# Thirty-two experts of 64 slots each become sixteen pairs that share 64 slots

## The chip, the cores and the metric

The kernel runs on one core of one Trainium2 chip. The core has five engines with a queue of instructions each: TensorE (PE; the loads of its stationary operand are shown apart, as PEld), VectorE (DVE), ScalarE (ACT), GpSimd (POOL) and SyncE (SP, which here issues the weight loads). Sixteen DMA engines move data between memory (HBM) and the core. A matmul writes into PSUM, from where VectorE or ScalarE fetches the result; all else lives in SBUF, 128 partitions of it. The metric is the device time of the whole program in microseconds. Before the change three runs took 1750.53, 1749.68 and 1748.38 us; the median is 1749.68 us.

## The reference

Two transformer blocks over 256 tokens of 1024 features. Block 1 is a mixer (mLSTM and gMLP), a cross attention and a mixture of 32 experts; block 2 has two layers, each with three mixers (a long convolution through a spectrum, gated linear attention, pooling) and a feed-forward part. The change is within the mixture of experts. Cut to what matters:

```python
def hier_moe(h, w_rg, b_rg, w_re, b_re, w_gate, w_up, w_down):
    p_group = jax.nn.softmax(h @ w_rg + b_rg)               # 4 groups of 8 experts
    p_top, g_idx = lax.top_k(p_group, 1)                    # each token goes to one group
    e_logits = (h @ w_re + b_re).reshape(T, 4, 8)           # ... and there
    e_top, e_local = lax.top_k(e_logits[own group], 2)      # to two experts
    weights = p_top * jax.nn.softmax(e_top)
    expert_id = g_idx * 8 + e_local
    ...
    y = (silu(xb @ w_gate[e]) * (xb @ w_up[e])) @ w_down[e] # the tokens xb of expert e
    return sum over a token's two experts of weights * y
```

The gate and up matrices of an expert are 1024 x 512, its down matrix is 512 x 1024, all fp32. All 32 experts have to be read, 201 MB, whatever the routing; 512 places (256 tokens, two experts each) are spread over them. Experts j and j + 16 are never in the same group, so no token goes to both.

## The kernel before

*Weights.* Each weight is used as hi + lo, two parts of 12 significant bits, in matmuls of the type fp32r. The experts' weights come as 192 loads of 1 MiB (raw, 128 x 2048), issued by SyncE, 9 of which can be in SBUF at once. A load is two chunks of 1024 columns. For each chunk ScalarE makes the hi part (whi, line 450) and VectorE the lo part (wlo, line 451, raw - whi). There are 5 buffers for hi parts and 4 for lo parts (NH, NL in the code), so that splits run at most five chunks ahead of TensorE. A load's place comes free when both its chunks are split.

*Slots.* Each expert has 64 slots. `rank` counts for every token how many tokens before it go to the same expert; that rank is its slot. Tokens beyond the 64th would be dealt with in a loop over all tokens, `beyond`, which makes no trips where all have a slot. `chosen` makes the one-hot Dm of token and slot for four experts on VectorE (line 849); `features` gathers with it 128 features of the tokens in those slots, for four experts at once, on TensorE (line 861), and ScalarE copies them into XT (line 864). The stationary operand of an expert's matmul is 128 features x 128: 64 slots of the token's hi part and 64 of its lo part. So one pass of whi and one of wlo gives rows 0 to 63 from the hi tokens and rows 64 to 127 from the lo tokens, and the two halves are added later.

*An expert* has 12 chunks, one a step: 4 for gate, 4 for up (`up`, lines 938 and 939), 4 for down (`down`, lines 954 and 955), with four matmuls of 512 columns each. Gate goes into a PSUM tile `misc`, of which there are two; ScalarE copies its lower half (z, line 885), VectorE adds the upper (line 887), and ScalarE makes SiLU of it twice, for both halves of g (line 891). Up goes into the other `misc` tile and VectorE multiplies it into g (line 895). `fold` adds the two halves of g and transposes in one go: four matmuls with a constant of stacked identity matrices (line 902), into a PSUM tile `tp` (also two); ScalarE and VectorE split that into at, hi and lo (lines 906 and 908). Down runs over at into two `tp` tiles, each copied to ye by ScalarE (line 913). `combine` takes ye back to the tokens: for each token tile and each half of the features one fp32 matmul (line 919) with DT, the weights of tokens in slots, accumulating in the four `acc` tiles over all experts. DT comes from `weighted`: VectorE multiplies Dm by the tokens' weights (Dw, line 873), TensorE transposes four 128 x 128 blocks (line 878), ScalarE copies (line 880).

*The order* is written out by hand. Each piece of work is a Python generator; `plan[step]` lists what is started at a step, a generator yields the number of steps until its next part, and `go_on` runs at each step those that are due, ahead of the step's four matmuls. `WHEN` and `DOWN` are tables of the steps: the features of the next four experts, their slots and weights, and one step of block 2's filters for nearly every expert (24 such steps, lines 1265 to 1290; all but four of them beside the experts). Gate and up of expert e are followed by down of expert e - 1, whose fold is started in step 2 of expert e; the combinations of expert e - 2 stand in steps 4 to 7.

All engines keep this order within the mixture of experts. What stands before it (its norm and the router) and after it (the last sums, two norms and block 2) is ordered by the same program in both kernels.

Of the kernel before, what the change touches and what calls it, by code (L numbers as in the profile page):

```python
# [22 lines left out]
F32 = mybir.dt.float32  # L23
# [8 lines left out]
P = 128  # L32
D = 1024
S = 256
# [45 lines left out]
# after which expert's first products an expert's last one follows: the next one's, but for those of the end,  # L80
# so that no expert's middle is waited for there
DOWN = lambda e: () if e in (0, NE - 2) else (e - 1,) if e < NE - 1 else (NE - 3,) if e == NE - 1 else (NE - 2, NE - 1)
# which of four experts, and which of its 12 steps: for 128 features of the next four each, their slots, their
# weights; and the steps for the filters of block 2
WHEN = dict(features=((1, 1), (1, 4), (1, 5), (1, 7), (3, 5), (3, 6), (3, 7), (4, 0)), chosen=(0, 2),
            weighted=((1, 8), (1, 9)), filters=(7, 7, 8, 2))
def _constants():
    """Tables by where they are needed, and what is where in them."""
# [5 lines left out]
        "cst": dict(ident=np.eye(P), fold=np.concatenate([np.eye(SLOTS)] * 2), slot=np.arange(SLOTS)[None] - BIG,  # L94
# [17 lines left out]
def _tables():  # L112
    """Constants of the second block that depend on its shapes alone."""
# [35 lines left out]
def _short(a):  # L149
    """Rounded to 12 significant bits."""  # L150
# [5 lines left out]
# tables of numbers of at most 12 significant bits  # L156
# [6 lines left out]
def _prepare(i):  # L163
    """Only layout: what the program reads, by name."""
# [32 lines left out]
    gu = np.stack([i["w_gate"][0], i["w_up"][0]], 1).reshape(NE, 2, 4, 2, P, 512)  # L197
    o["w_egu"] = _pairs(gu.transpose(0, 1, 2, 4, 3, 5).reshape(NE * 8, P, 1024))
    dn = i["w_down"][0].reshape(NE, 2, 2, P, 2, 512)
# [44 lines left out]
# ------------------------------------------------------------------- program  # L244

class Kernel:
# [13 lines left out]
    def weights(self, name, n, parts=None):  # L260
        """Chunk n of a weight as hi + lo, each of 12 significant bits."""
# [19 lines left out]
    def load(self):  # L281
        """The next load of the stream."""
# [11 lines left out]
    def ahead(self, n):  # L294
        """The first n chunks of the stream, split."""
# [8 lines left out]
    def constants(self, name, pool, w=0):  # L304
        """A table of constants, or the first columns of it (the rest is to be loaded by load_rest)."""
# [29 lines left out]
    def room(self, pool, tags):  # L335
        """Tiles for the parts of a chunk: one of both, or one of each (None: the usual one)."""
# [25 lines left out]
    def dense_t(self, xT, name, chunks, consume):  # L362
        """Columns of those chunks (128 each, at most two): consume(psum[128, n, 256])."""
# [9 lines left out]
    # ---- norms and transposes  # L373
# [7 lines left out]
    def squares(self, halves):  # L381
        """Sum of squares over both halves, as two columns."""
# [7 lines left out]
    def rsqrt(self, v, w=1):  # L390
        """v^-1/2 of a [128, w]."""
# [4 lines left out]
    def inv_norm(self, ss):  # L396
        """(sum + n eps)^-1/2: the inverse rms over sqrt(n) = 32."""
# [4 lines left out]
    def gained(self, x, g, out, n):  # L402
        """out = 32 x g, half n."""
# [3 lines left out]
    def to_T(self, src, hi, lo, t, k0=0, n=8):  # L407
        """src [128 tok, n * 128] of token tile t -> hi, lo [128, k0:k0+n, tok]; without lo, hi is the whole."""
# [16 lines left out]
    def norm(self, gname, pool, tag, g=None):  # L425
        """Tiles for rms_norm(x) g as hi, lo [128, 8, tok], and what fills them from a token tile."""
# [21 lines left out]
    def split(self, hi, lo, src):  # L448
        """hi + lo = src, each of 12 significant bits."""
# [3 lines left out]
    # ---- everything  # L453
# [37 lines left out]
    # ---- block 1: mixer, cross attention  # L491

    def block1(self, outer, moe):
# [3 lines left out]
        with ExitStack() as ctx:  # L497
# [33 lines left out]
            # gates: i_f at 0.., i_b at 32.., f_f at 64.., f_b at 96..  # L531
# [40 lines left out]
            # q, k: [128 of the head, head, tok]  # L572
# [16 lines left out]
            # E[s, t] = exp(u_s - M_t) where s reaches t  # L589
# [53 lines left out]
            # output gate and gu wait in y for what they multiply  # L643
# [9 lines left out]
            # gMLP  # L653
# [39 lines left out]
            # memory side of the cross attention does not wait for the mixer  # L693
# [22 lines left out]
            for e in range(NE + 1):  # L716
                if e < NE:
                    self.stream.extend(("w_egu", 4 * e + n) for n in range(4))
# [949 lines left out]
```

## Time and profile before

| | |
|---|---|
| runs | 1750.53, 1749.68, 1748.38 us |
| span of the profiled execution | 1747.4 us |
| TensorE busy in the span | 1689.9 us, 97% |
| VectorE | 1310.1 us, 75% |
| ScalarE | 1185.6 us, 68% |
| HBM traffic | 415.96 MB, mean 238 GB/s |
| mixture of experts, first gate matmul to last down matmul | 260.7 to 839.8 us, 579.1 us |

The profile is of one execution; its span of 1747.4 us lies 2.3 us under the median of the runs. A row of the timeline gives the start, the duration, the engine, the line, the operation, the result and what it is made from, and the shape; [in brackets] stands the idle time ahead of it and what ended that. Each fp32 matmul (lines 902 and 919) has two records, "x2" for one. Matmuls are pipelined: the next one starts before the record of the last one ends, so what one costs is read from the distance of two starts rather than from its duration. In the table of stretches a busy time stands for each engine, then the granted clock of TensorE as a share of 2.4 GHz, then the mean busy share of the DMA engines and what they moved.

### The profile page before, as it was taken

To read this page: it belongs to the slowest core of one execution; us is meant where nothing else is said; L and a number is where in the kernel's file an instruction comes from. 1 tells how busy PE (TensorE), PEld (TensorE's weight loads), DVE (VectorE), ACT (ScalarE), POOL (GpSimd) and SP (SyncE) were. 2 spreads that over 40 slices of the span, in tenths; PEclk is the share of its full clock that TensorE was granted. 3 is DMA by queue.
4 is the path that set the end of the run, shared out by engine and by line. 5 is a ranking of instruction groups with operands and counts; after the bars stand their busy time and mean duration, and the time that the engine had idled before them with its cause. 6 is when DMAs were issued, how large, how long until landed. Compare 5 with 4: busy or idle time off the path is not lost. (4 is left out here: it accounts for less than half of the span.)

```text
span 1747.4 us, 25396 instructions
## 1 busy us (share of the span) xinstructions
PE 1689.9 (97%) x9401; PEld 1421.2 (81%) x9401; DVE 1310.1 (75%) x1697; ACT 1185.6 (68%) x1672; POOL 30.4 (2%) x47
## 2 busy tenths in 40 slices
PE   7999978999999999999899999999999999999998
PEld 6898866777777777777589987899878998789986
DVE  7976568889888989999558867677655786667763
ACT  7865439889888889999557655555545765555552
POOL 1000000000000000000000000000000000000000
PEclk9999989999999999999999999999999999999999
DMA  8645537989899999998566456455656645645551
GB/s 286 210 165 192 192 140 271 354 337 362 333 344 350 358 346 369 372 388 335 175 211 222 147 187 215 149 184 185 212 178 210 233 142 188 202 152 183 185 192 69
DMA packets 94451, 415.96 MB, mean 238 GB/s; under 512 B 12324, under 2 KB 18868, under 8 KB 68468
## 3 DMA queue, kind: packets, MB, share of 16 engines
q1 hardware_dynamic: 89220, 405.91, 65.4%
q0 software_dynamic: 864, 6.29, 1.0%
q10 hardware_dynamic: 4240, 2.10, 0.4%
q8 instruction: 75, 1.23, 0.3%
q14 instruction: 52, 0.43, 0.1%
HBM read 411.12 MB, written 3.15 MB: 237 GB/s over the span
## 5 line engine op out<-in xcount | busy, mean ns | idle before, releaser
L451 DVE TENSOR_TENSOR wlo<-raw,whi 128x1024 fp32r<-128x1024 f32 x709 | 851.6, 1221 | 234.4 <-PE acc L328 82.9
L450 ACT ACTIVATE whi<-raw 128x1024 fp32r<-128x1024 f32 x711 | 733.0, 1054 | 203.4 <-PE acc L329 119.9
L332 PE MATMUL acc<-hl,whi 128*128 128x256 f32 x1024 | 290.1, 283 | 0.0
L333 PE MATMUL acc<-hh,wlo 128*128 128x256 f32 x1024 | 290.1, 283 | 0.0
L331 PE MATMUL acc<-hh,whi 128*128 128x256 f32 x1024 | 289.9, 283 | 0.0
L938 PE MATMUL misc<-whi,XT 128*128 128x512 f32 x512 | 241.3, 471 | 2.1 <-DVE z L887 1.3
L939 PE MATMUL misc<-wlo,XT 128*128 128x512 f32 x512 | 203.4, 397 | 2.5 <-DVE wlo L451 2.1
L331 PEld LDWEIGHTS acc<-hh,whi 128*128 128x128 f32 x1024 | 196.7, 192 | 0.1
L332 PEld LDWEIGHTS acc<-hl,whi 128*128 128x128 f32 x1024 | 196.7, 192 | 0.0
L333 PEld LDWEIGHTS acc<-hh,wlo 128*128 128x128 f32 x1024 | 196.7, 192 | 0.0
L939 PEld LDWEIGHTS misc<-wlo,XT 128*128 128x128 f32 x512 | 97.1, 190 | 44.4 <-issue 15.8
L919 PE MATMUL acc<-ye,DT 128*128 128x512 f32 x256 | 129.5, 592 | 0.0
L938 PEld LDWEIGHTS misc<-whi,XT 128*128 128x128 f32 x512 | 96.9, 189 | 39.6 <-issue 21.6
L327 PE MATMUL acc<-whi,hh 128*128 128x512 f32 x288 | 113.5, 395 | 0.6 <-ACT hh L418 0.5
L328 PE MATMUL acc<-wlo,hh 128*128 128x512 f32 x288 | 113.5, 395 | 0.1
L329 PE MATMUL acc<-whi,hl 128*128 128x512 f32 x288 | 112.8, 392 | 0.0
L954 PE MATMUL tp<-whi,at 128*128 128x512 f32 x256 | 110.1, 430 | 1.5 <-ACT XT L864 1.2
L955 PE MATMUL tp<-wlo,at 128*128 128x512 f32 x256 | 100.6, 393 | 0.4 <-DVE wlo L451 0.4
L327 PEld LDWEIGHTS acc<-whi,hh 128*128 128x128 f32 x288 | 54.5, 189 | 12.8 <-ACT hh L418 1.2
L329 PEld LDWEIGHTS acc<-whi,hl 128*128 128x128 f32 x288 | 54.5, 189 | 11.9 <-DVE hl L419 0.8
L328 PEld LDWEIGHTS acc<-wlo,hh 128*128 128x128 f32 x288 | 54.4, 189 | 11.3 <-DVE wlo L451 0.5
L954 PEld LDWEIGHTS tp<-whi,at 128*128 128x128 f32 x256 | 48.1, 188 | 18.0 <-issue 4.2
(459 smaller groups left out, 2847.9 us busy)
## 6 DMA issues: line engine op xcount, KB each, us to landing
raw<-in_w_egu SPq DMA_DIRECT2D x128, 1024.0 KB
raw<-in_w_ed SPq DMA_DIRECT2D x64, 1024.0 KB
raw<-in_w_up SPq DMA_DIRECT2D x80, 512.0 KB
raw<-in_w_gate SPq DMA_DIRECT2D x48, 512.0 KB
raw<-in_w_down SPq DMA_DIRECT2D x44, 512.0 KB
raw<-in_w_qk SPq DMA_DIRECT2D x24, 512.0 KB
raw<-in_w_out SPq DMA_DIRECT2D x24, 512.0 KB
raw<-in_w_br SPq DMA_DIRECT2D x24, 512.0 KB
```

The costliest lines, as they stand in the source:

```text
L327: mm(out, xh, wh, start=start, stop=False)
L328: mm(out, xh, wl, start=False, stop=False)
L329: mm(out, xl, wh, start=False, stop=stop)
L331: mm(out, wh, xh, start=start, stop=False)
L332: mm(out, wh, xl, start=False, stop=False)
L333: mm(out, wl, xh, start=False, stop=stop)
L450: self.nc.scalar.activation(hi, src, AF.Copy)
L451: self.nc.vector.tensor_sub(lo, src, hi.bitcast(F32))
L919: mm(sums[t][n], DT[e // 4][:, e % 4, t * P:(t + 1) * P], Y[e, n], start=e == 0, stop=e == NE - 1)
L938: mm(p, l, wh[:, c], start=h == k == 0, stop=False)
L939: mm(p, l, wl[:, c], start=False, stop=h == 3 and k == 1)
L954: mm(p, l, wh[:, c], start=h == k == 0, stop=False)
```

## The change

Experts j and j + 16 make a pair. The pair has one set of 64 slots: the tokens of the first member come first, those of the second behind them (in `rank`, two more matmuls add the first member's count to the second member's ranks, and `mine` marks which of the rows belong to the first). Each member's XT holds its own tokens in their slots and zeros in the other slots. So gate of the first and gate of the second can accumulate into one `misc` tile over 8 chunks, up likewise, and one copy, one sum, two SiLU and one product serve both. `fold` gets a moving operand of 128 columns instead of 64, F: the stacked identities with only the first member's rows, and with only the second's. VectorE makes F for each pair (lines 915 and 916), two steps ahead of the fold's matmuls. So `at` has both members' hidden features, zeros in the other's slots, and down of both accumulates in one `misc` tile (before: `tp`) over 4 chunks for each half of the features. Two ye copies and four combinations follow for each pair. `weighted` makes Dw for two pairs at a time, with small VectorE operations from the slot numbers and two small tables (rp, wp), two steps before its transposes instead of six. A step of the plan is still one chunk; a pair has 24 steps, and a load is still 1 MiB, two chunks. The loads come in the new order of the chunks. The numbers of buffers NH, NL and the 9 places stay.

The diff, without what only removes comments:

```diff
+PAIRS = NE // 2
+MEMBERS = [m * PAIRS + j for j in range(PAIRS) for m in range(2)]
+WHEN = dict(features=((0, 6), (0, 9), (0, 12), (0, 15), (1, 14), (1, 16), (1, 18), (1, 20)), chosen=2,
+            weighted=(1, 4, 7, 10), filters=(8, 14), combine=(3, 5, 7, 9))
+DOWN = lambda j: (j - 1,) if j else ()
...
+            rp, wp = (a.tile([P, 2, PAIRS], F32, name=k) for k in ("rp", "wp"))
+            r2 = rk.rearrange("p t (j m) -> p t j m", m=2)
+            nc.vector.tensor_tensor(rp, r2[:, :, :, 0], r2[:, :, :, 1], op=OP.min)
+            nc.vector.tensor_add(wp, W[:, :, :PAIRS], W[:, :, PAIRS:])
...
+            def weighted(o, t, h):
+                Dw = a.tile([P, 2, 2, SLOTS], F32, name="Dw")
+                for n in range(2):
+                    j = 4 * o + 2 * h + n
+                    nc.vector.tensor_scalar(Dw[:, n], self.c["slot"][:, None, :].to_broadcast([P, 2, SLOTS]),
+                                            rp[:, t, j:j + 1], wp[:, t, j:j + 1], op0=OP.is_equal, op1=OP.mult)
+                yield 2
                 ps = self.tp()
-                for e in range(4):
-                    nc.tensor.transpose(ps[:, e * P:(e + 1) * P], Dw[:, e].rearrange("p i j -> p (i j)"), self.ident)
+                for n in range(2):
+                    nc.tensor.transpose(ps[:, n * P:(n + 1) * P], Dw[:, n].rearrange("p i j -> p (i j)"), self.ident)
                 yield 1
...
-            def fold(e):
-                g = G.pop(e)
+            def fold(j):
+                F = a.tile([P, 2, SLOTS], F32, name="F")
+                nc.vector.tensor_scalar(F[:, 0], self.c["fold"], mine[:, j:j + 1], None, op0=OP.mult)
+                nc.vector.tensor_sub(F[:, 1], self.c["fold"], F[:, 0])
+                yield 2
+                g = G.pop(j)
                 pt = self.tp()
                 for f in range(4):
-                    mm(pt[:, f * SLOTS:(f + 1) * SLOTS], g[:, f * P:(f + 1) * P], self.c["fold"], start=True, stop=True)
+                    mm(pt[:, f * P:(f + 1) * P], g[:, f * P:(f + 1) * P], F.rearrange("p m j -> p (m j)"),
+                       start=True, stop=True)
...
                 for i in range(2):
                     p = self.misc()
-                    for h in range(4):
+                    for s in range(8):
+                        m, h = divmod(s, 4)
                         go_on()
-                        wh, wl = self.weights("w_egu", 8 * e + 4 * i + h)
+                        wh, wl = self.weights("w_egu", 16 * j + 8 * m + 4 * i + h)
                         for k in range(2):
-                            l = XT[q][h][:, k, r].rearrange("p i j -> p (i j)")
+                            l = XT[q][h][:, k, 2 * r + m].rearrange("p i j -> p (i j)")
                             c = slice(k * 512, k * 512 + 512)
-                            mm(p, l, wh[:, c], start=h == k == 0, stop=False)
-                            mm(p, l, wl[:, c], start=False, stop=h == 3 and k == 1)
+                            mm(p, l, wh[:, c], start=s == k == 0, stop=False)
+                            mm(p, l, wl[:, c], start=False, stop=s == 7 and k == 1)
...
-                    p = self.tp()
-                    for h in range(2):
+                    p = self.misc()
+                    for s in range(4):
+                        m, h = divmod(s, 2)
                         go_on()
-                        wh, wl = self.weights("w_ed", 4 * e + 2 * n + h)
+                        wh, wl = self.weights("w_ed", 8 * j + 4 * m + 2 * n + h)
...
+                if j < PAIRS:
+                    plan[0].append(fold(j - 1))
+                if j == 1 or j % 4 == 3 and j < PAIRS - 1:
+                    for n, s in enumerate(WHEN["weighted"]):
+                        plan[s].append(weighted((j + 1) // 4, n // 2, n % 2))
...
+            plan[WHEN["combine"][2 * n + t]].append(combine(j - 2, t, n))
```

Two places of the order show how instructions move. The first is VectorE around the fold of one expert, in the second half of the stage, before the change; lines 451, 908, 887 and 895 are the lo part, the lo part of at, the gate's sum and the product with up.

```order
L451 TENSOR_TENSOR wlo<-raw,whi 128x1024 x8
L908 TENSOR_TENSOR at<-tp,at 128x4x64
L451 TENSOR_TENSOR wlo<-raw,whi 128x1024
L887 TENSOR_TENSOR z<-misc,z 64x512
L451 TENSOR_TENSOR wlo<-raw,whi 128x1024 x3
L895 TENSOR_TENSOR g<-g,misc 128x512
```

The same place after it, for one pair; lines 455, 929, 901 and 909 are the same operations, 915 and 916 make F.

```order
L909 TENSOR_TENSOR g<-g,misc 128x512
L455 TENSOR_TENSOR wlo<-raw,whi 128x1024 x9
L915 TENSOR_SCALAR F<-cst,mine 128x64
L916 TENSOR_TENSOR F<-cst,F 128x64
L455 TENSOR_TENSOR wlo<-raw,whi 128x1024 x3
L929 TENSOR_TENSOR at<-tp,at 128x8x64
L455 TENSOR_TENSOR wlo<-raw,whi 128x1024 x5
L901 TENSOR_TENSOR z<-misc,z 64x512
```

Between two products with up there are now 24 lo parts instead of 12, and the two operations for F stand three lo parts ahead of at's subtraction, which follows the fold's matmuls.

The second place is TensorE between combinations, in the middle of the stage. Before, one chunk, that is four weight matmuls (lines 938 and 939), stand between two combinations (line 919):

```order
L919 MATMUL acc<-ye,DT 128x512
L938 MATMUL misc<-whi,XT 128x512
L939 MATMUL misc<-wlo,XT 128x512
L938 MATMUL misc<-whi,XT 128x512
L939 MATMUL misc<-wlo,XT 128x512
L919 MATMUL acc<-ye,DT 128x512
```

After, with lines 960 and 961 for the weight matmuls and 940 for the combination:

```order
L940 MATMUL acc<-ye,DT 128x512
L960 MATMUL misc<-whi,XT 128x512
L961 MATMUL misc<-wlo,XT 128x512
L960 MATMUL misc<-whi,XT 128x512
L961 MATMUL misc<-wlo,XT 128x512
L960 MATMUL misc<-whi,XT 128x512
L961 MATMUL misc<-wlo,XT 128x512
L960 MATMUL misc<-whi,XT 128x512
L961 MATMUL misc<-wlo,XT 128x512
L940 MATMUL acc<-ye,DT 128x512
```

Now two chunks of weights, eight matmuls, stand between two combinations instead of one chunk with four, and there are four combinations in 24 chunks instead of four in 12.

## Rows read from the trace of the kernel before

**Rows 1.** The page: its first line and TensorE's line of busy time.

```profile
span 1747.4 us, 25396 instructions
...
PE 1689.9 (97%) x9401; PEld 1421.2 (81%) x9401; DVE 1310.1 (75%) x1697; ACT 1185.6 (68%) x1672; POOL 30.4 (2%) x47
```

**Rows 2.** Stretches: us, busy PE, PEld, DVE, ACT, POOL, clock, DMA share, GB/s.

```profile
260.70:298.00 37.30, 32.29 (x149) 25.64 (x149) 28.38 (x30) 33.02 (x44) 0.00 (x0) 0.90 0.73 261
298.00:633.10 335.10, 329.22 (x1526) 247.95 (x1525) 293.47 (x297) 292.74 (x388) 0.00 (x0) 1.00 0.93 347
633.10:799.10 166.00, 164.97 (x737) 125.29 (x736) 158.04 (x156) 158.92 (x204) 0.00 (x0) 1.00 0.97 375
799.10:839.80 40.70, 40.01 (x161) 27.96 (x160) 37.25 (x37) 33.96 (x42) 0.00 (x0) 1.00 0.57 234
380.00:390.00 10.00, 10.00 (x44) 7.37 (x43) 7.49 (x9) 6.59 (x8) 0.00 (x0) 1.00 1.00 396
430.00:440.00 10.00, 10.00 (x49) 7.52 (x48) 9.09 (x9) 9.92 (x14) 0.00 (x0) 1.00 1.00 391
780.00:805.00 25.00, 25.00 (x111) 19.26 (x109) 24.82 (x25) 23.94 (x30) 0.00 (x0) 1.00 1.00 398
281.60:285.00 3.40, 3.40 (x13) 3.02 (x14) 1.90 (x3) 1.79 (x3) 0.00 (x0) 0.50 0.86 318
```

**Rows 3.** Stretches of line 885 alone: busy ScalarE and count of copies, then as above.

```profile
298.00:633.10 335.10, 10.71 (x18) 1.00 0.93 347
633.10:799.10 166.00, 5.95 (x10) 1.00 0.97 375
```

**Rows 4.** TensorE's timeline around two combinations: start, us, operation.

```profile
510.98 1.02 PE L919 MATMUL acc<-ye,DT 128*128 128x512 f32 x2
511.44 0.79 PE L938 MATMUL misc<-whi,XT 128*128 128x512 f32 x1
512.07 0.39 PE L939 MATMUL misc<-wlo,XT 128*128 128x512 f32 x1
...
512.77 1.02 PE L919 MATMUL acc<-ye,DT 128*128 128x512 f32 x2
```

**Rows 5.** TensorE's timeline around a fold.

```profile
504.77 0.39 PE L939 MATMUL misc<-wlo,XT 128*128 128x512 f32 x1
505.00 1.00 PE L902 MATMUL tp<-cst,g 128*128 128x64 f32 x8
505.81 0.48 PE L938 MATMUL misc<-whi,XT 128*128 128x512 f32 x1
506.12 0.39 PE L939 MATMUL misc<-wlo,XT 128*128 128x512 f32 x1
```

**Rows 6.** VectorE's timeline in a late expert.

```profile
781.41 9.34 DVE L451 TENSOR_TENSOR wlo<-raw,whi 128x1024 fp32r<-128x1024 f32 x8
790.66 0.42 DVE L908 TENSOR_TENSOR at<-tp,at 128x256 fp32r<-128x256 f32 x1
791.00 1.22 DVE L451 TENSOR_TENSOR wlo<-raw,whi 128x1024 fp32r<-128x1024 f32 x1
792.13 0.67 DVE L887 TENSOR_TENSOR z<-misc,z 64x512 f32<-64x512 f32 x1
792.73 2.34 DVE L451 TENSOR_TENSOR wlo<-raw,whi 128x1024 fp32r<-128x1024 f32 x2
```

**Rows 7.** Groups by line and shape, 298 to 799.1 us: count, busy, mean, idle before.

```profile
L939 PEld LDWEIGHTS misc<-wlo,XT 128*128 128x128 f32 x448 | 84.5, 189 | 41.5 <-issue 14.8 <-DVE wlo L451 12.2 <-DVE Dm L849 1.0
...
L873 DVE TENSOR_TENSOR Dw<-Dm,W 128x512 f32<-128x512 f32 x13 | 8.9, 685 | 0.0
L878 PE MATMUL tp<-cst,Dw 128*128 128x128 f32 x56 | 8.8, 280 | 3.3 <-ACT DT L880 3.2
...
L1285 DVE MEMSET fk<- 1x128 f32 x6 | 1.0, 165 | 1.0 <-ACT fk L1281 0.9
```

**Rows 8.** TensorE's timeline, two waits within the first two experts.

```profile
275.81 0.47 PE L938 MATMUL misc<-whi,XT 128*128 128x512 f32 x1 [1.30 <-DVE z L887]
...
280.09 0.50 PE L861 MATMUL tp<-Dm,hh 128*128 128x256 f32 x2 [2.19 <-DVE Dm L849]
```

More of the change, by code (lines that the diff above doesn't have):

```diff
@@ L93, in _constants @@
     tables = {
-        "cst": dict(ident=np.eye(P), fold=np.concatenate([np.eye(SLOTS)] * 2), slot=np.arange(SLOTS)[None] - BIG,
+        "cst": dict(ident=np.eye(P), fold=np.concatenate([np.eye(SLOTS)] * 2), row=(s % SLOTS)[:, None], slot=np.arange(SLOTS)[None] - BIG,
                     idx=np.arange(NE)[None] - BIG, tri=s[:, None] < s[None, :]),
@@ L941, in up, with down @@
+                            mm(p, l, wl[:, c], start=False, stop=s == 7 and k == 1)
+                        for work in plan[8 * i + s]:
                             start(work)
-                    start(gated(e, p) if i else gate(e, p))
-            def down(e, plan):
-                at = AT.pop(e)
+                    start(gated(j, p) if i else gate(j, p))
+            def down(j, plan):
+                at = AT.pop(j)
                 for n in range(2):
-                    p = self.tp()
-                    for h in range(2):
+                    p = self.misc()
+                    for s in range(4):
+                        m, h = divmod(s, 2)
@@ L956, in down @@
-                        for work in plan[8 + 2 * n + h]:
+                            mm(p, l, wh[:, c], start=s == k == 0, stop=False)
+                            mm(p, l, wl[:, c], start=False, stop=s == 3 and k == 1)
+                        for work in plan[16 + 4 * n + s]:
                             start(work)
-                    start(result(e, n, p))
+                    start(result(j, n, p))
             def flush():
@@ L966, in moe @@
             todo = deque(twice(w) for w in spectra[:1] * 12 + spectra[1:] * 12)
-            last = NE // 4 - 1
+            last = PAIRS // 2 - 1
             start(chosen(0))
@@ L972, in moe @@
             go_on()
[L973 to L976 removed]
+            for j in range(PAIRS + 1):
+                q, r = divmod(j, 2)
+                plan = [[] for n in range(24)]
+                if j == 0:
                     for k in range(2, 8):
                         plan[k // 2 - 1].append(features(0, k))
[L979 to L994 removed]
@@ new lines, in moe @@
+                elif j < PAIRS:
+                    plan[0].append(fold(j - 1))
+                if j == PAIRS - 1:
+                    plan[16].append(fold(j))
+                if j == 1 or j % 4 == 3 and j < PAIRS - 1:
+                    for n, s in enumerate(WHEN["weighted"]):
+                        plan[s].append(weighted((j + 1) // 4, n // 2, n % 2))
+                if q < last:
+                    if r == 0:
+                        plan[WHEN["chosen"]].append(chosen(q + 1))
+                    for k, (rr, s) in enumerate(WHEN["features"]):
+                        if rr == r:
+                            plan[s].append(features(q + 1, k))
@@ L995, in moe @@
+                if 1 < j < PAIRS:
                     for n in range(2):
                         for t in range(2):
-                            plan[4 + 2 * n + t].append(combine(e - 2, t, n))
-                if e and len(todo) > KEEP:
-                    if len(todo) == 12:
-                        next(spectra[1])
-                    plan[WHEN["filters"][r]].append(todo.popleft())
-                if e < NE:
-                    up(e, plan)
-                for d in DOWN(e):
-                    if e == NE:
-                        plan = [[] for n in range(12)]
-                        for n in range(2):
-                            plan[8 + n].extend(combine(d - 1, t, n) for t in range(2))
-                        if d == NE - 1:
-                            plan[11].extend(combine(d, t, 0) for t in range(2))
-                        if d == NE - 2:
-                            plan[8].append(fold(NE - 1))
+                            plan[WHEN["combine"][2 * n + t]].append(combine(j - 2, t, n))
@@ new lines, in moe @@
+                for s in WHEN["filters"]:
+                    if 0 < j < PAIRS and len(todo) > KEEP:
+                        if len(todo) == 12:
+                            next(spectra[1])
+                        plan[s].append(todo.popleft())
+                if j < PAIRS:
+                    up(j, plan)
+                else:
+                    for n in range(2):
+                        plan[17 + n].extend(combine(j - 2, t, n) for t in range(2))
+                    plan[23].extend(combine(j - 1, t, 0) for t in range(2))
@@ L1013, in moe @@
+                for d in DOWN(j):
                     down(d, plan)
@@ L1020, in moe @@
             xg = [self.junk.tile([P, D], F32, name="xn", bufs=2) for t in range(2)]
-            ws = [[a.tile([P, 512], F32, name="w", tag=("g", "Dw")[t], bufs=2) for n in range(2)] for t in range(2)]
+            ws = [a.tile([P, 2, 512], F32, name="w", tag="at", bufs=2) for t in range(2)]
+            ws = [[w[:, n] for n in range(2)] for w in ws]
             def squares(t, n, src, to):
@@ L1055, in moe @@
             for t in range(2):
-                next(combine(NE - 1, t, 1))
+                next(combine(PAIRS - 1, t, 1))
             with tc.manual_schedule(engines=engines - {mybir.EngineType.PE}):
@@ L1067, in moe, with rank @@
             return hT
-    def rank(self, a, hh, hl, A, W, rk):
+    def rank(self, a, hh, hl, A, W, rk, mine):
         nc = self.nc
```

112 lines of the change are left out of this document (46 added, 66 removed).

## The prediction, made before the changed kernel was run

> **What bounds the kernel now.** I began with the page: the span is 1747.4 us and TensorE is busy for 97% of it [rows 1]. That share alone says little, because the ends of matmuls are modelled, so the next view was the table of stretches. It shows the expert stage cut at points that I chose from the timeline: the first gate matmul of expert 0 (260.7), of expert 2 (298.0), of expert 20 (633.1), of expert 30 (799.1), and the end of the last down matmul (839.8) [rows 2]. The reader is to see that TensorE has nearly no free time in any of these stretches, and that VectorE, ScalarE and the DMA share stand close behind it: 0.88, 0.87 and 0.93 in the second stretch, 0.95, 0.96 and 0.97 in the third. The copies of the gate's lower half, one for each expert, count the experts [rows 3]: 18 in 335.1 us, so 18.6 us each or 37.2 us for two, and 10 in 166.0 us, so 16.6 us each or 33.2 us for two. The second stretch is slower since nearly every expert in it carries one step of block 2's filters; the difference, 2.0 us, is the price of such a step.
>
> That TensorE sets this pace is seen in the timeline of its matmuls: they stand without gaps, 0.23 us apart [rows 5]. Its waits for the split weights are small, 12.2 us in 501 [rows 7].
>
> **What leaves TensorE.** The expert matmuls of gate, up and down stay, 48 for each expert; two experts now write into one PSUM tile but take as many matmuls as before. What goes is the work per expert behind them.
> - Combination: from one of these matmuls to the next there lie 1.79 us and four weight matmuls [rows 4]. Less 4 x 0.23, one costs 0.87 us. There are 4 for each expert, now 4 for each pair: 64 x 0.87 = 55.7 us go.
> - Fold: from the matmul before it to the second one after it 1.35 us pass, with two matmuls of 0.23 in it, so about 0.9 us [rows 5]. Its four matmuls have 128 moving columns now instead of 64. No row shows that form; the bounds are 0.9 us (if each record is held by the load of its weights, as the 8 records for 64 columns seem to be) and 1.8 us (twice). I take 0.9, since the 512 columns of the combination cost 0.87 and a quarter of that four times is again 0.87. 16 x 0.9 = 14.4 us go.
> - Transposes of the slot weights: 56 keep TensorE busy for 8.8 us [rows 7], 0.16 each; 32 of 64 go, 5 us.
>
> Together 75 us, or 4.7 us for each pair. At TensorE's pace alone a pair would take 37.2 - 4.7 = 32.5 us with filters and 33.2 - 4.7 = 28.5 without. This is more than the others can follow, so each is to be asked what is late next.
>
> **What the others need for a pair.** *VectorE*: at full load eight splits took 9.25 us, 1.16 each, a sum of 128x512 or 64x512 0.60, and the 128x256 subtraction 0.34 [rows 6]. In that stretch it was busy for 24.82 of 25.00 us [rows 2], so these are its limits. After: 24 splits 27.8; one z, one g and one at (now 512 columns) 1.8; half a Dm 0.3; and four small operations of 64 or 128 columns (two for F, on average two for Dw). Between the 0.165 us of a memset and the 0.685 us of the old Dw [rows 7] I take 0.25, nearer to the lower row since they have an eighth or a quarter of the columns: 1.0 (bounds 0.7 and 2.7). Sum 30.9, with filters 31.3. Before it was 2 x (13.9 + 0.6 + 0.6 + 0.34) + 0.9 = 31.8: the change takes little from VectorE.
> *ScalarE* drops one z (0.6), two SiLU halves (1.25), two ye (1.2) and some of the rest: from 0.96 x 33.2 = 31.8 to about 28.5. It isn't late next.
> *The weight stream*: 12 loads of 1 MiB, 12.58 MB for each pair; with filters 335.1 x 347 GB/s over 9 pairs = 12.92 MB. At a DMA share of 1.00 the rows show 391, 396 and 398 GB/s [rows 2]. So at least 12.92 / 393 = 32.9 us early and 12.58 / 398 = 31.6 us late.
>
> The Trainium skill ("DMA: Bandwidth & Descriptors", Specifications) gives an HBM limit of about 358 GB/s for each core. By that, a pair could take no less than 12.58 / 358 = 35.1 us (an estimate from that page), and the third stretch would be impossible as it is; this trace does not agree, with 375 GB/s over 166 us and 398 over 25 us [rows 2]. I therefore go by the rows.
>
> **New waits.** Fold now needs F, which VectorE makes two steps ahead. In VectorE's order F stands behind the split of the chunk four ahead, and that split needs a low-part buffer (there are 4) which TensorE frees with the chunk just done. So F is ready 1.22 + 2 x 0.25 = 1.7 us after the end of chunk 0, and TensorE is there after chunk 1, 0.92 us later: a wait of 0.8 us, in which the next gate and up matmuls stand queued behind the fold. The least is 0, if fold's neighbours delay TensorE, the most 3 x 1.16 + 0.5 = 4.0 us, if VectorE is fully behind. Of the four Dw transposes of four pairs, three have a fold, a combination or a filter step in front that covers the same delay; one does not. That is 5 waits of 0.8 in four pairs, 1.0 us each, and 0.2 for the others' remains. VectorE itself loses little: it goes on with the next split.
>
> **The sum.**
> - Start: seven instead of five rank matmuls and six more tiny VectorE operations ahead of the first slots: +1.0 (between 0 and 2).
> - Pair 0: the old stretch of 37.3 us held experts 0 and 1 with the down of expert 0 (16 x 0.23 = 3.7), a fold (0.9), a filter step (2.0) and two waits of 1.30 and 2.19 us, for the only free gate tile and for the late Dm [rows 8]. All these are moved or gone: the second gate now has 16 chunks of time, and Dm is asked for at step 2. 37.3 - 10.1 = 27.2.
> - Pairs 1 to 10, two filter steps each: TensorE 32.5 + 1.2 = 33.7, the stream 32.9, VectorE 31.3. I take 33.7: 337.
> - Pairs 11 to 15: the stream 31.6, VectorE 30.9, TensorE 29.7. Three so close don't fit into one another exactly: 32.0, so 160.
> - The last down: 32 matmuls 7.4, four combinations 3.5: 10.9.
>
> 260.7 + 1.0 + 27.2 + 337 + 160 + 10.9 = 796.8 instead of 839.8: 43 us earlier. After that both programs have the same instructions in the same order (the final combinations, norms and all of block 2). The profiled execution would have a span of 1704.4; the median of the runs, 1749.68, lies 2.3 us above the span, so I forecast **1706.7 us**, some 2.5% less.
>
> **Rivals.**
> *A. The forecast*: stream, VectorE and TensorE share the bound. 0.60.
> *B. The stream can't keep its peaks.* If 375 GB/s, the mean of the third stretch, is all that it holds over long times, pairs take 12.92 / 375 = 34.5 and 12.58 / 375 = 33.5 us: 345 + 168 instead of 337 + 160, 1723 us. For it speaks that a share of 0.97 is near full; against it that TensorE set the pace there and that the share reached 1.00 only later, with more bytes. 0.13; in 0.04 of that it holds the old 347 too, and hardly 3 us are won. The 358 GB/s of the Trainium skill would lead to the latter.
> *C. The new waits are long.* If F and the uncovered Dw come 2 to 3 us late, each early pair takes 35.3 or more and each late one 32.8: some 1726 us. For it speaks that VectorE has little lead to lose; against it that a waiting TensorE lets VectorE catch up. 0.12.
> *D. Everything fits.* Early 32.9, late 31.0, pair 0 24: 1747.4 - 63 + 2.3 = 1687 us. 0.08.
> *E. The clock falls, and it is slower.* Now TensorE rarely waits; then it must. After the two waits of 1.30 and 2.19 us the granted clock was 0.50 for 3.4 us, and over the first 37.3 us it was 0.90 on average [rows 2, 8], which is 3.7 us of full clock lost. If every pair lost that through waits gathered at one place, 16 x 3.7 = 59 us would be lost and 1766 us result; it becomes slower from 2.7 us for each pair on. Against it: in the two long stretches the clock is 1.00 although TensorE waits there in small pieces. 0.05.
> *F. It doesn't do what it says*: if over 64 tokens fell on a pair, the loop for late tokens would run over all 32 experts, hundreds of microseconds. The reference's own routing puts at most 48 on a pair with its first seed. 0.02.
>
> **Range and chances.** From D to somewhat beyond C: 1688 to 1730 us; within A alone 1696 to 1716. Differences under 0.2%, 3.5 us, can't be told from none. Faster 0.90 (A, C, D and most of B), the same 0.04 (B's rest), slower 0.06 (E, F).
>
> **What would show it.** Combination matmuls halved to 64 (128 records), 16 z copies; from the first gate matmul to the last down matmul about 536 us instead of 579; a DMA share of 0.97 or more between pair 1 and pair 15 at 380 to 398 GB/s; TensorE's busy share there below 0.97, its waits going to the low parts and to F; VectorE at 0.92 or more. I am wrong if the DMA share stays near 0.93 with TensorE waiting for F or Dw (C), if the share is 1.00 at 360 to 375 GB/s (B), or if the granted clock in the stage is below 0.98 (E).

## The result and the profile after

The changed kernel takes 1760.21 us (median of 4 runs, 1758.11 to 1762.66) against 1749.88 us of the kernel before beside it: 1.0059 times as long, 95% interval 1.0044 to 1.0073. It is some 10 us slower, where 43 us less had been forecast. The profiled execution has a span of 1759.4 us. The first line of its page and TensorE's line answer to [rows 1]:

```profile
span 1759.4 us, 24723 instructions
...
PE 1653.8 (94%) x9115; PEld 1391.7 (79%) x9115; DVE 1293.6 (74%) x1702; ACT 1138.4 (65%) x1576; POOL 30.3 (2%) x47
```

TensorE has 286 matmul records less and is busy for 36.1 us less, and yet the program is longer: the time is in waits. The table of stretches answers to [rows 2]; it is cut at the first gate matmul of pairs 0, 1, 11 and 15 and at the end of the last down.

```profile
261.00:286.40 25.40, 22.21 (x106) 17.39 (x106) 19.03 (x18) 24.03 (x31) 0.00 (x0) 0.95 0.76 278
286.40:669.50 383.10, 345.59 (x1515) 260.76 (x1513) 316.43 (x333) 297.21 (x373) 0.00 (x0) 0.94 0.90 335
669.50:803.10 133.60, 120.41 (x505) 88.75 (x504) 122.32 (x126) 115.60 (x138) 0.00 (x0) 0.97 0.97 372
803.10:851.80 48.70, 42.78 (x162) 31.11 (x161) 39.48 (x40) 34.87 (x40) 0.00 (x0) 0.93 0.66 261
```

Pairs 1 to 10 take 38.3 us each; two experts took 37.2 before. The granted clock is 0.94 there, where it was 1.00. Nothing is full: TensorE 0.90, VectorE 0.83, the DMA share 0.90. What TensorE waits for, over the whole stage:

```profile
PE tp L921 <- DVE F L916: 47.3, 16, 3.6
PE tp L891 <- DVE Dw L886: 5.0, 5, 1.6
PE misc L978 <- DVE wlo L455: 3.9, 8, 0.8
```

Line by line: engine, tile and line, what it waited for, us in all, how often, the longest. The fold waits for F in each of the 16 pairs, 3 us each time. From the start of pair 5 (440.8) on, TensorE's timeline has only one long wait:

```profile
442.83 0.40 PE L961 MATMUL misc<-wlo,XT 128*128 128x512 f32 x1
446.18 1.13 PE L921 MATMUL tp<-F,g 128*128 128x128 f32 x8 [2.96 <-DVE F L916]
447.07 0.48 PE L960 MATMUL misc<-whi,XT 128*128 128x512 f32 x1
...
449.02 1.02 PE L940 MATMUL acc<-ye,DT 128*128 128x512 f32 x2
...
451.75 1.02 PE L940 MATMUL acc<-ye,DT 128*128 128x512 f32 x2
```

VectorE's timeline at the same place shows why, and ScalarE's what the wait does further on:

```profile
435.31 10.30 DVE L455 TENSOR_TENSOR wlo<-raw,whi 128x1024 fp32r<-128x1024 f32 x9
445.53 0.25 DVE L915 TENSOR_SCALAR F<-cst,mine 128x64 f32<-128x64 f32 x1
445.81 0.22 DVE L916 TENSOR_TENSOR F<-cst,F 128x64 f32<-128x64 f32 x1
445.95 1.22 DVE L455 TENSOR_TENSOR wlo<-raw,whi 128x1024 fp32r<-128x1024 f32 x1
448.34 2.36 DVE L455 TENSOR_TENSOR wlo<-raw,whi 128x1024 fp32r<-128x1024 f32 x2 [1.17 <-ACT at L927]
```

```profile
442.48 2.95 ACT L454 ACTIVATE whi<-raw 128x1024 fp32r<-128x1024 f32 x3
447.35 0.60 ACT L927 ACTIVATE at<-tp 128x512 fp32r<-128x512 f32 x1 [1.92 <-PE tp L921]
```

VectorE makes nine lo parts without a pause, 1.14 us each, for the last four chunks of the down part and the first five of the next gate; TensorE needs only 4 x 0.23 = 0.92 us for such a chunk, since no combination stands between them. So VectorE loses its lead, that is, the chunks by which its lo parts are ahead of TensorE (four buffers allow four). TensorE comes to the fold at 443.2 (442.83 + 0.40), while three lo parts, for chunks that it needs only after the fold, still stand ahead of F, the first of them nearly done. Then ScalarE stands at the copy of the fold's result, the hi parts behind it stand too, and VectorE after them: the wait goes round to the engine that caused it.

Pair 5 kept its full clock. In pair 4, within the same wait (404.83 to 407.79), the clock fell to the lower of its two levels (0.50 is 1.2 GHz). TensorE's timeline, and the stretch at that level:

```profile
404.44 0.39 PE L961 MATMUL misc<-wlo,XT 128*128 128x512 f32 x1
407.79 2.05 PE L921 MATMUL tp<-F,g 128*128 128x128 f32 x8 [2.96 <-DVE F L916]
```

```profile
406.75:413.55 6.80, 5.76 (x17) 4.85 (x18) 3.90 (x7) 3.36 (x5) 0.00 (x0) 0.50 0.99 378
```

This happened at 12 of the 16 waits, for 3.4 or 6.8 us. By the table of stretches 0.06 x 383.1 + 0.03 x 133.6 + 0.07 x 48.7 = 30 us of full clock were lost; a part of them lies within the waits, where TensorE had nothing to do (1.04 us in the stretch shown). "TensorE: Matmul & The Clock Gate" (Part 1: The HAM clock gate) of the Trainium skill says that this clock follows how busy TensorE has just been. The rows agree: each of the twelve falls stands at a wait of about 3 us, while the long stretches of before without such waits stand at 1.00 [rows 2].

Behind the last down matmul both programs take the same: 1747.4 - 839.8 = 907.6 us before, 1759.4 - 851.8 = 907.6 after.

### The profile page after: what moved, and what is told of

Same layout as the page of the kernel before. It is cut to its first block, busy times and chain, and to the rows that moved or that the text cites. A ratio compares the mean times of both kernels' runs of the same rounds, so it can differ in the third digit from the quotient of the medians.

```text
span 1759.4 us, 24723 instructions
## 1 busy us (share of the span) xinstructions
PE 1653.8 (94%) x9115; PEld 1391.7 (79%) x9115; DVE 1293.6 (74%) x1702; ACT 1138.4 (65%) x1576; POOL 30.3 (2%) x47
## 5 line engine op out<-in xcount | busy, mean ns | idle before, releaser
L961 PE MATMUL misc<-wlo,XT 128*128 128x512 f32 x512 | 213.9, 418 | 1.1 <-DVE wlo L455 1.1
L961 PEld LDWEIGHTS misc<-wlo,XT 128*128 128x128 f32 x512 | 102.0, 199 | 41.0 <-DVE wlo L455 11.9
L960 PEld LDWEIGHTS misc<-whi,XT 128*128 128x128 f32 x512 | 102.4, 200 | 35.6 <-issue 13.2
L978 PE MATMUL misc<-wlo,at 128*128 128x512 f32 x256 | 104.9, 410 | 3.9 <-DVE wlo L455 3.9
L977 PE MATMUL misc<-whi,at 128*128 128x512 f32 x256 | 103.2, 403 | 0.0
L921 PE MATMUL tp<-F,g 128*128 128x128 f32 x128 | 25.1, 358 | 47.3 <-DVE F L916 47.3
L978 PEld LDWEIGHTS misc<-wlo,at 128*128 128x128 f32 x256 | 48.7, 190 | 24.5 <-DVE wlo L455 14.9
L940 PE MATMUL acc<-ye,DT 128*128 128x512 f32 x128 | 66.6, 607 | 0.0
L921 PEld LDWEIGHTS tp<-F,g 128*128 128x128 f32 x128 | 21.5, 254 | 53.9 <-issue 47.1
```

Source lines behind the costliest of these rows:

```text
L960: mm(p, l, wh[:, c], start=s == k == 0, stop=False)
L961: mm(p, l, wl[:, c], start=False, stop=s == 7 and k == 1)
L977: mm(p, l, wh[:, c], start=s == k == 0, stop=False)
L978: mm(p, l, wl[:, c], start=False, stop=s == 3 and k == 1)
```

## The experiments

Theory Q: the loss is F's place in VectorE's queue, as a wait and by the clock that falls behind it. Rival V: VectorE or the weight stream bounds a pair anyway, and a wait removed in one place returns in another. Rival T: the clock falls for another reason than the wait. All runs below are of the changed kernel with the edit shown, save the last; ratios are to the kernel before.

**F early.** The two operations for F start at step 12 of their own pair:

```diff
+            def masked(j):
+                FS[j] = F = a.tile([P, 2, SLOTS], F32, name="F")
...
+                yield 1
...
+            def fold(j):
                 yield 2
+                F = FS.pop(j)
...
+                if j < PAIRS:
+                    plan[12].append(masked(j))
```

> The two operations that make F are started in step 12 of the pair's own gate and up steps, 14 steps ahead of the fold instead of 2; nothing else moves. Theory Q (place in the queue): in the changed kernel's trace the fold waits 2.96 us for F in nearly every pair, because F stands behind splits in VectorE's order at the point where VectorE has no lead, and the granted clock falls to 0.50 behind most of these waits (58 us in twelve stretches). With F early both go: waits 47 us, clock 58 x 0.5 = 29 us at most, and the sum of the prediction is what remains: 1705 to 1715 us, granted clock 1.00 in the stage from the second pair on, no wait for F above 0.3 us. Rival V (the others are late anyway): VectorE or the weight stream bounds a pair at 37 us whatever the place of F; the wait then reappears before matmuls of low parts, 1745 to 1760 us.

Measured: 1713.68 us, 0.9789 (0.9773 to 0.9805). No fold waits for F any more. 46.5 us come back, as Q has it. V fails as the account of the loss; a part of what it says is seen, for TensorE's other waits in the stage grew from 12.4 to 24.9 us, above all those for Dw. The stretches of pairs 1 to 10 and pairs 11 to 15, and TensorE's largest waits:

```profile
287.40:631.80 344.40, 328.68 (x1513) 247.40 (x1513) 312.10 (x333) 293.69 (x372) 0.00 (x0) 0.99 0.95 372
631.80:788.10 156.30, 149.43 (x629) 108.83 (x628) 152.66 (x157) 142.11 (x169) 0.00 (x0) 0.99 0.98 400
```

```profile
PE tp L891 <- DVE Dw L886: 11.8, 9, 2.1
PE misc L982 <- DVE wlo L455: 6.5, 14, 0.8
PE tp L925 <- DVE g L909: 2.8, 2, 1.9
```

**The wait filled.**

```diff
                 pt = self.tp()
+                for f in range(12):
+                    mm(pt, hh[:, 0, :P], hh[:, 0, :512], start=True, stop=True)
                 for f in range(4):
```

> F is made as late as in the changed kernel; ahead of the four fold matmuls TensorE gets twelve matmuls of 512 columns that write into the fold's PSUM tile and need nothing late (12 x 0.233 = 2.8 us, about the length of the wait; their result is overwritten by the fold). It separates the wait's length from the clock. Theory Q: TensorE is busy through the wait, the granted clock stays 1.00, the pairs stay about 3 us longer than need be: the 58 us at half clock are given back, up to 29 us, so 1730 to 1740 us. Rival T (the clock falls for lack of work in the stage as a whole, not for the wait): the clock still falls in about twelve stretches, 1755 to 1765 us. Rival V: 1755 to 1765 us too, but with a clock of 1.00.

Measured: 1739.20 us, 0.9937 (0.9921 to 0.9954). In pairs 1 to 15 the clock stays at its upper level, and 0.7 us of waits for F are left in all:

```profile
285.90:649.60 363.70, 354.28 (x1634) 268.63 (x1633) 315.54 (x333) 296.15 (x373) 0.00 (x0) 1.00 0.93 352
649.60:815.10 165.50, 163.47 (x705) 122.18 (x704) 153.68 (x159) 142.59 (x169) 0.00 (x0) 1.00 0.97 378
```

```profile
PE tp L923 <- DVE F L916: 0.7, 1, 0.7
```

So T fails: with work in place of the wait, the clock doesn't fall. Of the 46.5 us, 1760.2 - 1739.2 = 21 are the clock's and 1739.2 - 1713.7 = 25.5 the waits'. The fillers cost TensorE about as long as the waits did, 47 us; less is felt, because without them TensorE waits elsewhere: its other waits sum to 24.9 us with F early and to 11.9 here. That accounts for 13 of the 21.5 us. Some 4 more are the clock's, which from pair 1 on stood at 0.50 for 7.8 us with F early and never here; the rest stays open.

**The fold two steps later**, `yield 4` for `yield 2` in `fold`.

> F is made where it was; the fold's matmuls stand four steps behind it instead of two. Theory Q: two more steps give TensorE 2 x 0.93 us of other work while VectorE catches up, so the wait shrinks from 2.96 to about 1.1 us: 16 x 1.9 = 30 us, and if the clock does not fall behind 1.1 us another 25: 1705 to 1730 us. Rival V: 1750 to 1760 us, the waits turn up at the low parts of the two chunks in between.

Measured: 1718.18 us, 0.9811 (0.9794 to 0.9827). The waits for F went to 1.2 us in all, less than the 1.1 each that was expected. Those for Dw grew to 18.1 us, up to 3.8 us in one, and the clock fell behind the long ones. Q holds for F, and for Dw the same mechanism showed.

**F on GpSimd**, `nc.gpsimd` for `nc.vector` in its two operations.

> F is made at the same step as in the changed kernel, but on GpSimd, whose queue is empty there. Theory Q: what counts is the queue, not the moment of issue, so the wait goes as in the first kernel: 1705 to 1715 us, if two operations of 128x64 take GpSimd under 1.9 us (two chunks of TensorE). If GpSimd needs longer, a wait of that length less 1.9 us is left. Rival V: 1745 to 1760 us.

Measured: 1710.13 us, 0.9765 (0.9745 to 0.9785). No fold waits for F. But the expectation took the wrong ground: in GpSimd's timeline F is made as soon as its buffer is free, some 30 us ahead, not at the step of its plan, and it isn't quick:

```profile
431.09 5.04 POOL L915 TENSOR_SCALAR F<-cst,mine 128x64 f32<-128x64 f32 x1 [29.85 <-PE tp L921]
436.21 0.32 POOL L916 TENSOR_TENSOR F<-cst,F 128x64 f32<-128x64 f32 x1
```

So this run shows again that F must be early, and not that GpSimd would be in time two steps ahead.

**Dw where VectorE has a lead**: F early, and `weighted=(6, 8, 10, 12)` for `(1, 4, 7, 10)`.

> F early as in e1_mask_early, and the slot weights Dw started at steps 6, 8, 10 and 12 of their pair instead of 1, 4, 7 and 10. In the trace of e1_mask_early nine waits for Dw are left, 11.8 us, three of them of 2.0 to 2.1 us at the first of the four, where VectorE still has no lead; the clock fell behind two of them for 3.41 us. Theory Q: behind the first combinations VectorE has a lead, so of the 11.8 us under 4 remain, and the two falls of the clock go (3 us): 1701 to 1707 us. Rival V: the pairs wait for low parts or for loads instead, 1710 to 1715 us.

Measured: 1714.51 us, 0.9802 (0.9787 to 0.9817): no gain. Dw is still waited for, 11.1 us in ten waits, the long ones now mostly of about 1.2 us rather than 2.1. The expectation was wrong in that a lead makes two steps enough. VectorE's and TensorE's timelines at one such place:

```profile
376.06 1.23 DVE L455 TENSOR_TENSOR wlo<-raw,whi 128x1024 fp32r<-128x1024 f32 x1 [0.26 <-PE misc L965]
377.69 0.49 PE L891 MATMUL tp<-cst,Dw 128*128 128x128 f32 x2 [0.79 <-DVE Dw L886]
```

VectorE stood idle ahead of the split that Dw follows, until TensorE was done with the chunk that frees its buffer. So it had its full lead, and TensorE still waited 0.79 us (three times), the value that the forecast had worked out for F. Where the two operations for F now stand ahead of Dw as well, it waited 1.22 us (three times).

**Combinations twice**, on top of the last: each combination matmul issued a second time.

> As e5_weights_later, but each combination matmul is issued twice (64 more; what the experts add is counted twice in the output). It prices the forecast's largest term, 64 combinations of 0.87 us. If TensorE sets the pace in pairs 1 to 10 (about 33.5 us in e1_mask_early) and the weight stream in pairs 11 to 15 (29.7 us at a DMA share of 1.00): 10 x 3.5 + 5 x 2.5 + 3.5 in the last down = 51 us more than e5_weights_later, so 1750 to 1758 us. If VectorE or the stream sets the pace early too, TensorE has room for part of it: at most 25 us more, 1720 to 1730 us.

Measured: 1749.71 us, 1.0004 (0.9994 to 1.0015), 35.2 us more than the last, between the two cases. The stretches of pairs 1 to 10 and 11 to 15 grew from 344.7 to 371.3 and from 156.6 to 166.0 us:

```profile
285.80:657.10 371.30, 359.17 (x1587) 263.90 (x1585) 315.11 (x335) 296.05 (x373) 0.00 (x0) 0.99 0.91 345
657.10:823.10 166.00, 161.91 (x669) 116.00 (x668) 153.24 (x157) 142.35 (x169) 0.00 (x0) 1.00 0.97 376
```

In an early pair 2.7 of the 3.5 added microseconds are felt, in a late one 1.9. Of the 2.7 some 0.25 are the clock's, which stood at 0.50 for 10.2 us in the early pairs here and for 5.3 us in the last run. TensorE is the main bound of the early pairs, not their only one.

**Fold at step 8**, `plan[6].append(fold(j - 1))` for `plan[0]`.

> The changed kernel with F and fold six steps later: F after step 6, the fold's matmuls at step 8, still two steps apart. Theory Q in its narrower form (VectorE has no lead over TensorE at the end of a down part, where TensorE needs 0.93 us for a chunk and VectorE 1.16, and gets one behind the combinations): at step 8 two steps are enough, the wait is 0.8 us or less, as the forecast had it for every place: 1703 to 1715 us. If two steps are too few anywhere (F stands behind the split of the chunk four ahead), the wait stays above 2 us: 1745 to 1760 us.

Measured: 1736.03 us, 0.9918 (0.9901 to 0.9936), between the two cases. TensorE's waits:

```profile
PE tp L921 <- DVE F L916: 18.2, 13, 3.4
PE tp L891 <- DVE Dw L886: 16.2, 8, 3.4
```

Behind the combinations most waits for F are 1.2 to 1.35 us instead of 2.96, so the place matters as the narrower form of Q says. They aren't 0.8 or less, because VectorE's lead isn't full there in most pairs. The timelines of VectorE and TensorE at such a wait, and then at one of three folds that waited only 0.1 us:

```profile
480.09 4.62 DVE L455 TENSOR_TENSOR wlo<-raw,whi 128x1024 fp32r<-128x1024 f32 x4
484.63 0.25 DVE L915 TENSOR_SCALAR F<-cst,mine 128x64 f32<-128x64 f32 x1
485.28 1.13 PE L921 MATMUL tp<-F,g 128*128 128x128 f32 x8 [1.31 <-DVE F L916]
...
522.66 1.23 DVE L455 TENSOR_TENSOR wlo<-raw,whi 128x1024 fp32r<-128x1024 f32 x1 [0.27 <-issue]
523.34 1.02 PE L940 MATMUL acc<-ye,DT 128*128 128x512 f32 x2
524.46 1.13 PE L921 MATMUL tp<-F,g 128*128 128x128 f32 x8
```

In the first, VectorE works up to F without a pause: the split that F follows starts at about 480.09 + 3 x 1.14 = 483.5, 1.8 us after the end of the chunk that frees its buffer (481.70). In the second, VectorE stood idle ahead of that split, which starts 0.1 us after its buffer came free (522.56), and the fold begins 0.1 us behind the combination. So with a full lead and a combination in between two steps are enough; most folds at step 8 find VectorE 1.2 to 1.8 us short of that. All three folds with the full lead and a combination in between stand behind a wait of 2.79 us for Dw, in which VectorE could catch up.

**Filters spread over fifteen pairs**: as *Dw where VectorE has a lead*, with `WHEN["filters"][:1 + (j % 3 == 1)]`.

> As e5_weights_later, with block 2's twenty filter steps spread over pairs 1 to 15 (two in every third pair, one in the others) instead of two in each of pairs 1 to 10. If TensorE bounds the early pairs and the weight stream the late ones, as in e1_mask_early, each pair comes to about 31.5 to 32 us, 15 x 31.7 = 476 instead of 484 us: 5 to 10 us less than e5_weights_later, 1693 to 1700 us. If the sum of the stream bounds both parts, no change: 1700 to 1706 us.

Measured: 1721.67 us, 0.9849 (0.9835 to 0.9863), 7 us more instead of 5 to 10 less. The late pairs took 167.5 instead of 156.6 us: 1.8 us for each of six more steps, where 31.5 to 32 us a pair, at most 160, had been expected. The early ones won nothing (344.0 instead of 344.7) although six steps left: a wait for Dw of 2.8 us and one of 2.3 us for a filter's weights that came late by DMA, each with a fall of the clock, stood in their place. A filter step is no burden that can be moved for free: each place has its own waits.

**Room for both**: F early, Dw four steps ahead of its transposes, and the last fold behind the product that it needs.

```diff
-            weighted=(1, 4, 7, 10), filters=(8, 14), combine=(3, 5, 7, 9))
+            weighted=(1, 7, 13, 18), filters=(8, 14), combine=(3, 5, 7, 9))
...
                                             rp[:, t, j:j + 1], wp[:, t, j:j + 1], op0=OP.is_equal, op1=OP.mult)
-                yield 2
+                yield 4
...
-                    plan[16].append(fold(j))
+                    plan[17].append(fold(j))
```

> F early as in e1_mask_early; the slot weights Dw are started at steps 1, 7, 13 and 18 with their transposes four steps behind instead of two, and the last pair's fold one step later, behind the product that it waits for. In e1_mask_early 11.8 us of waits for Dw and one of 1.9 us for that product are left, and the clock falls behind three of these waits. Theory Q: four steps cover VectorE's delay wherever it stands, so these waits go: 9 to 12 us less than e1_mask_early, 1702 to 1705 us. Rival V: since in e5_weights_later the waits only got shorter and the time stayed, TensorE isn't what sets the pace there, and the time stays at 1711 to 1715 us.

Measured: 1700.98 us, 0.9715 (0.9700 to 0.9729), the shortest of all, 50 us under the kernel before and 12.7 under F early, where 9 to 12 had been expected. 0.9 us of waits for Dw are left, against 11.8 with F early alone, so V fails here too. That row, and the stretches of pair 0, pairs 1 to 10, pairs 11 to 15 and the last down:

```profile
PE tp L891 <- DVE Dw L886: 0.9, 3, 0.5
...
260.40:285.70 25.30, 22.48 (x105) 17.68 (x105) 18.99 (x18) 23.99 (x31) 0.00 (x0) 0.94 0.76 282
285.70:622.80 337.10, 326.82 (x1514) 247.55 (x1514) 312.06 (x335) 292.68 (x373) 0.00 (x0) 0.99 0.96 379
622.80:775.50 152.70, 148.88 (x633) 107.74 (x632) 151.56 (x157) 141.61 (x169) 0.00 (x0) 1.00 1.00 412
775.50:786.80 11.30, 11.30 (x44) 7.90 (x43) 7.71 (x7) 5.20 (x7) 0.00 (x0) 1.00 0.01 2
```

**The wait alone, in the kernel before**: no pairing, only the fold's constant copied by VectorE two steps ahead (the fold's matmuls come to stand ahead of the matmuls of step 2 instead of behind them, as in the changed kernel).

```diff
+                F = a.tile([P, 512], F32, name="F", tag="z")[:, :SLOTS]
+                nc.vector.tensor_scalar(F, self.c["fold"], 1.0, None, op0=OP.mult)
+                yield 2
...
-                    plan[2].append(fold(e - 1))
+                    plan[0].append(fold(e - 1))
```

> The kernel before, with the one new wait alone: the fold's constant is copied by VectorE for each expert (128x64, one operation) two steps ahead of the fold's matmuls, as F is in the changed kernel; no pairing. Theory Q: the copy stands behind the split of the chunk four ahead here too. VectorE loses less lead over 4 down chunks than over 8, so the wait lies between the 1.2 us of e7_fold_at_8 and the 2.96 of the changed kernel: some 1.5 to 2.5 us for 31 experts, of which about half is felt (as between e1_mask_early and e2_wait_filled), 25 to 40 us, and 10 to 30 more where the clock falls: 1770 to 1810 us. If the wait hurts only because of the pairing (longer stretches without combinations), it is hidden here: 1749 to 1755 us.

Measured: 1842.36 us, 1.0529 (1.0513 to 1.0545), 92 us slower by one operation of 0.18 us per expert. TensorE's waits at the fold, line 905:

```profile
PE tp L905 <- DVE F L900: 30.7, 14, 3.0
PE tp L905 <- ACT DT L880: 10.6, 5, 2.8
PE tp L905 <- ACT XT L864: 10.2, 6, 2.4
PE tp L905 <- ACT whi L450: 8.0, 6, 1.3
```

They sum to 59.5 us. The rows name ScalarE for half of them, yet F ends these waits too: each of the 30 folds from 306.12 to 902.72 starts 0.15 us after the end of F, whatever its row names, as here:

```profile
437.76 0.19 DVE L900 TENSOR_SCALAR F<-cst 128x64 f32<-128x64 f32 x1
438.10 1.08 PE L905 MATMUL tp<-F,g 128*128 128x64 f32 x8 [1.33 <-ACT whi L450]
```

The expected wait per expert (1.5 to 2.5) is right, 59.5 / 30 = 2.0. Its price was not: the waits are felt whole rather than by half, and the clock falls with them. It was 0.94 over the 670.2 us of the stage, against 0.99 over 579.1 before, some 34 us of full clock; 59.5 and 34 account for the 92. That is 92 / 30 = 3.1 us for each wait, close to the 46.5 / 16 = 2.9 of the changed kernel, so the pairing is not needed for the loss.

## Why the prediction was wrong

**The step that failed is "New waits".** It put F 1.7 us behind the end of chunk 0 and the fold's wait at 0.8 us, and gave 4.0 as the most, "if VectorE is fully behind". The wait was 2.96 us in pair after pair, 47.3 us in all. The value holds for a VectorE with its full lead, and the only ground that the prediction has for one is the average over a pair (30.9 us of work, less than TensorE's). But a wait is set by the lead at its place: by the forecast's own rows a lo part takes 1.16 us and a chunk without combinations 4 x 0.23 = 0.92, so the eight down chunks and the two gate chunks ahead of the fold take 10 x 0.24 = 2.4 us, two lo parts, from the lead. With a full lead at the start of the down part, 0.8 + 2.4 = 3.2 us would have been the estimate, near the 2.96 measured. For a full lead the prediction's working is borne out: 0.79 us for Dw where VectorE had it (*Dw where VectorE has a lead*), and 0.1 us for F where a combination stood in between (*Fold at step 8*).

**Two rivals were one.** Rival C had waits of 2 to 3 us and 1726 us; rival E had the clock, from "waits gathered at one place". The long wait is such a place, so C brings E. Taken apart by the two runs with F early and with the wait filled, C's waits cost 25.5 us and E's clock 21. Both signs that the prediction names came: a DMA share of 0.90 with TensorE waiting for F, and a clock of 0.94. E's direction was right, with a chance of 0.05, and its size per pair (3.7 us) too large: 21 / 16 = 1.3 us. The 3.7 us were misread, too: about half of them come from the first 3.8 us of that stretch, ahead of the two waits, where the clock was still at its lower level:

```profile
260.70:264.50 3.80, 3.80 (x13) 2.95 (x12) 2.01 (x2) 3.58 (x5) 0.00 (x0) 0.50 0.57 195
```

**The rest of the sum stood.** The fold takes 447.07 - 446.18 = 0.89 us (forecast 0.9), a combination 451.75 - 449.02 - 8 x 0.23 = 0.89 (forecast 0.87). The tail is unchanged. Stretch by stretch (after, the last down starts at 840.7):

| | forecast | after | room for both |
|---|---|---|---|
| first gate matmul | 261.7 | 261.0 | 260.4 |
| pair 0, us | 27.2 | 25.4 | 25.3 |
| pairs 1 to 10 | 337 | 383.1 | 337.1 |
| pairs 11 to 15 | 160 | 171.2 | 152.7 |
| last down | 10.9 | 11.1 | 11.3 |
| median | 1706.7 | 1760.2 | 1701.0 |

With both waits gone pairs 1 to 10 come to the forecast's 337 us. So close a match is partly luck: the forecast's 33.7 us a pair hold 1.2 us of waits for F and Dw, of which next to nothing is left there; other waits and a clock of 0.99 stand in their place. That TensorE alone sets 33.7 us is too simple, too: of 3.5 us added to it at most 2.7 were felt. Rival D's sum was off: its own terms (32.9, 31.0 and 24 us) take 16 us from the forecast and give 1690 us, not 1687.

**One term was too cautious.** For the late pairs 398 GB/s was taken as the stream's peak. With room for both it moved 412 GB/s over 152.7 us at a DMA share of 1.00, with VectorE busy for 151.56 us, so 30.5 us a pair instead of 32.0. So rival B fails. The prediction weighed only the lower of two figures of the Trainium skill: "Perfetto Trace Analysis" (Roofline) says that a core that runs alone can go beyond its share of 358 GB/s, up to about 435 GB/s of its DMA engines. The 412 GB/s agrees with that.

## What to carry to other kernels

A small operation on a busy engine is paid by its place in the queue, not by its length: ask how far ahead that engine is there, in the stage where the consumer runs fastest, and put what depends on nothing late many steps ahead. A new wait of some 3 us on TensorE should be priced with the clock that can fall behind it, not as a separate risk. When a change comes out slower, take its parts apart: the pairing was worth 50 us once F and Dw stood early enough, and in the kernel before one such operation, placed late, cost 92 us without any pairing.

## What was not expected of the hardware

One core drew 412 GB/s for 153 us. GpSimd took between 0.45 and 5.64 us (median 2.65) for the same multiplication of 128x64 elements that VectorE does in 0.25. Waits of the same 2.96 us came with 0, 3.4 or 6.8 us at half clock: the same wait has no fixed price.
